# Grouped-query attention on one core: a quarter of the exponentials moves from VectorE to ScalarE, with a check of the row sums and a branch at the end

## The chip, the cores and the metric

The kernel runs on one core of a Trainium2 chip. The metric is device time in microseconds (us); a kernel is run several times and the median counts. The profile is one execution recorded by the hardware profiler: its span runs from the first to the last instruction. The engines are TensorE (PE; its weight loads are listed as PEld), VectorE (DVE), ScalarE (ACT), GpSimd (POOL) and SyncE (SP).

## The reference

Q is 8 x 512 x 32 x 64 (batch, sequence, heads, dimension), K and V have 8 heads of the same length and dimension; all are float32 draws from a unit normal. Four query heads share one key and value head.

```
scores  = einsum('bhqd,bhkd->bhqk', Q, K_expanded) / sqrt(64)
weights = exp(scores - max(scores))
weights = weights / (sum(weights) + 1e-10)
output  = einsum('bhqk,bhkd->bhqd', weights, V_expanded)
```

## The kernel before, in words

There are 32 units: a unit is one batch entry and two key/value heads. GpSimd loads its K, Q and V three units ahead (`emit_load_k` L89, `emit_load_q` L75, `emit_load_v` L101, with a column of ones behind V, L99), converting to bf16. TensorE transposes K and Q of the next unit (L118, L130) into a PSUM buffer, and VectorE copies them out (L120, L134), in three of the four slots of a unit.

A unit has four slots, so there are 128; a slot `p` is one pair of query heads. For each of four chunks `kc` of 128 keys, `emit_scores_chunk` takes a PSUM buffer `s_unit` (128 x 1024 float32, a ring of three, which the transposes share) and makes two matmuls into it (L169), one for each head; the two use different halves of the rows of the array. Then the exponential of the 1024 columns is written as bf16 to the tile `pt`. No row maximum is subtracted. Three of the four chunks go to ScalarE's Exp (L186). The chunk `kc == 1` goes to VectorE (L177): one multiply and add whose result, rounded to a 16-bit integer, is read as the bits of a bf16 number, which approximates the exponential.

`emit_pv_chunk` multiplies the weights of slot `p - 1` with V and accumulates in the single PSUM buffer `pv` (L206, 32 matmuls of 65 columns in a slot); column 65 is the row sum, from the column of ones. `emit_norm` takes reciprocals of the row sums (L223, tile `inv`) and writes the scaled output to `o_sb` (L224). A unit's output is stored by GpSimd during the next unit (L149), the last one at the end.

The loop writes, for each slot: scores 0 and 1, values 0 and 1 of the slot before, scores 2 and 3, values 2 and 3, normalization, transposes. A scheduler orders the instructions of each engine by its own estimate; engines meet through semaphores, and a tile can be written again only when its last reader is done.

Of the kernel before, what the change touches and what calls it, by code (L numbers as in the profile page):

```python
# [10 lines left out]

FP32 = mybir.dt.float32
BF16 = mybir.dt.bfloat16
U16 = mybir.dt.uint16


@with_exitstack
def kernel(
# [7 lines left out]
    nc = tc.nc  # L26

    B, S, H, D = Q.shape
    KV = K.shape[2]
    HPG = H // KV  # L30
    SC = S // 128
# [3 lines left out]
    NSLOT = NU * 2 * NPAIR  # L35

    scale = 1.0 / math.sqrt(D)

    DVE_KC = 1

    SCHRAUD_C = 5.0
    LOAD_PREFETCH = 2
    STORE_DELAY = 2

    A_schr = (2.0 ** 7) / math.log(2.0) * scale
    B_schr = 127.0 * (2.0 ** 7) - SCHRAUD_C

    const_pool = ctx.enter_context(tc.tile_pool(name="const", bufs=1))
    qnat_pool = ctx.enter_context(tc.tile_pool(name="qnat", bufs=LOAD_PREFETCH + 2))
    knat_pool = ctx.enter_context(tc.tile_pool(name="knat", bufs=LOAD_PREFETCH + 2))  # L50
    v_pool = ctx.enter_context(tc.tile_pool(name="v", bufs=LOAD_PREFETCH + 2))
    qt_pool = ctx.enter_context(tc.tile_pool(name="qt", bufs=6))
    kt_pool = ctx.enter_context(tc.tile_pool(name="kt", bufs=3))
    pt_pool = ctx.enter_context(tc.tile_pool(name="pt", bufs=3))
    osb_pool = ctx.enter_context(tc.tile_pool(name="osb", bufs=STORE_DELAY + 2))
    misc_pool = ctx.enter_context(tc.tile_pool(name="misc", bufs=8))

    spsum_pool = ctx.enter_context(tc.tile_pool(name="spsum", bufs=3, space=bass.MemoryType.PSUM))
    pv_pool = ctx.enter_context(tc.tile_pool(name="pv", bufs=1, space=bass.MemoryType.PSUM))

    ident = const_pool.tile([128, 128], BF16)
    make_identity(nc, ident)

    def unit_bgp(u):
        return u // GP, u % GP
# [79 lines left out]
    def emit_store(u, split=False):  # L145
        b, gp = unit_bgp(u)
        h_base = 2 * gp * HPG
        o_sb = pending_stores.pop(u)
        nc.gpsimd.dma_start(  # L149
            out=out[b, :, h_base:h_base + 2 * HPG, :].rearrange(  # L150
                "(sc p) h d -> p sc h d", p=128
            ),
            in_=o_sb,
        )

    jobs = {}
    osb = {}

    def emit_scores_chunk(p, kc):
        st = jobs[p]  # L160
        u, g, i = st["u"], st["g"], st["i"]
        kt_all = trans[u]["kt"]
        qt_tile = trans[u]["qt"][g]
        pt_tile = st["pt"]
        pair_idx = st["pidx"]

        s_unit = spsum_pool.tile([128, 2, S], FP32, name="s_unit")
        for m in range(2):
            nc.tensor.matmul(  # L169
                s_unit[:, m, :],  # L170
                kt_all[64 * m:64 * m + 64, g, kc * 128:(kc + 1) * 128],
                qt_tile[64 * m:64 * m + 64, i, :],
                start=True,
                stop=True,
            )
        if kc == DVE_KC:
            nc.vector.tensor_scalar(  # L177
                out=pt_tile[:, kc, :, :].bitcast(U16),
                in0=s_unit[:, :, :],
                scalar1=float(A_schr),  # L180
                scalar2=float(B_schr),
                op0=mybir.AluOpType.mult,
                op1=mybir.AluOpType.add,
            )
        else:
            nc.scalar.activation(  # L186
                out=pt_tile[:, kc, :, :],
                in_=s_unit[:, :, :],
                func=mybir.ActivationFunctionType.Exp,
                scale=float(scale),  # L190
            )

    def emit_pv_chunk(p, kc):
        st = jobs[p]
# [19 lines left out]
    def emit_norm(p):  # L214
        st = jobs.pop(p)
        u, g, i = st["u"], st["g"], st["i"]
        if u not in osb:
            osb[u] = osb_pool.tile([128, SC, 2, NPAIR, 2, D], FP32, name="o_sb")
            pending_stores[u] = osb[u]
        o_sb = osb[u]  # L220
        o_psums = st["opsums"]
        inv = misc_pool.tile([128, 2, SC], FP32, name="inv")
        nc.vector.reciprocal(out=inv, in_=o_psums[:, :, :, D:D + 1])  # L223
        nc.vector.tensor_tensor(  # L224
            out=o_sb[:, :, g, i, :, :].rearrange("p qc m d -> p m qc d"),
            in0=o_psums[:, :, :, 0:D],
            in1=inv[:, :, :, None].to_broadcast((128, 2, SC, D)),
            op=mybir.AluOpType.mult,
        )
        if st["pidx"] == 2 * NPAIR - 1:  # L230
            osb.pop(u)
# [8 lines left out]
    for p in range(NSLOT + 1):  # L240
        real = p < NSLOT
        if real:
            u, pidx = divmod(p, 2 * NPAIR)
            g, i = divmod(pidx, NPAIR)
# [16 lines left out]
        if real:  # L261
            emit_scores_chunk(p, 0)
            emit_scores_chunk(p, 1)
# [3 lines left out]
        if real:  # L267
            emit_scores_chunk(p, 2)
            emit_scores_chunk(p, 3)
        if have_pv:  # L270
            emit_pv_chunk(p - 1, 2)
            emit_pv_chunk(p - 1, 3)
            emit_norm(p - 1)
# [3 lines left out]
    for w in sorted(pending_stores):  # L277
        emit_store(w, split=True)


# [1 line left out]
_INS = ['Q', 'K', 'V']  # L282
# [26 lines left out]
```

## Time and profile before

| what | value |
|---|---|
| median of 3 runs | 452.14 us (452.01 to 453.33) |
| span of the profiled execution | 449.0 us |
| between the span and the median of the runs | 3.1 us |
| TensorE, VectorE, ScalarE busy | 371.9, 326.0, 367.0 us |
| exponentials on ScalarE | 384, mean 1024 ns each |
| approximations on VectorE | 128, mean 1221 ns each |
| mean granted TensorE clock | 0.995 |

The profile states no other time of the profiled execution than its span; the 3.1 us are the difference of two columns of the table. In a group line the numbers are: busy time and mean duration of one, then the idle time of the engine before such instructions and what ended it. A wait line has the total, the number of waits and the longest. Timeline lines begin with start and length of a run of equal instructions.

### The profile page before, as it was taken

To read this page: it belongs to the slowest core of one execution; us is meant where nothing else is said; L and a number is where in the kernel's file an instruction comes from. 1 tells how busy PE (TensorE), PEld (TensorE's weight loads), DVE (VectorE), ACT (ScalarE), POOL (GpSimd) and SP (SyncE) were. 2 spreads that over 40 slices of the span, in tenths; PEclk is the share of its full clock that TensorE was granted. 3 is DMA by queue.
4 is the path that set the end of the run, shared out by engine and by line. 5 is a ranking of instruction groups with operands and counts; after the bars stand their busy time and mean duration, and the time that the engine had idled before them with its cause. 6 is when DMAs were issued, how large, how long until landed. Compare 5 with 4: busy or idle time off the path is not lost.

```text
span 449.0 us, 13535 instructions
## 1 busy us (share of the span) xinstructions
PE 371.9 (83%) x5888; PEld 219.5 (49%) x5888; DVE 326.0 (73%) x480; ACT 367.0 (82%) x385; POOL 219.0 (49%) x326
## 2 busy tenths in 40 slices
PE   2888888888888888888888888888888888888882
PEld 1445545555455455455554554554545545545541
DVE  1577787777787777778777778777778777777761
ACT  1688888888888888888888888888888888888881
POOL 9988556454456554446645445645445652200000
PEclk9999999999999999999999999999999999999998
DMA  9999999999999999999999999999999999212222
GB/s 90 151 160 213 206 173 148 159 126 121 168 173 147 156 140 113 160 176 149 158 154 110 145 172 165 148 156 128 122 169 172 147 155 157 36 80 96 95 95 93
DMA packets 143930, 63.78 MB, mean 142 GB/s; under 512 B 102912, under 2 KB 135680, under 8 KB 143872
## 3 DMA queue, kind: packets, MB, share of 16 engines
q0 software_dynamic: 143872, 62.93, 95.7%
q8 instruction: 46, 0.75, 0.7%
q14 instruction: 12, 0.10, 0.1%
HBM read 58.72 MB, written 33.55 MB: 206 GB/s over the span
## 4 chain that ended last, share of the span: by engine, by line
PE 65%; issue 13%; ACT 11%; POOL 7%; DMA 1%; ACTq 1%; DVE 0%; POOLq 0%
PE s_unit L169 30%; PE pv L206 28%; ACT pt L186 11%; PE s_unit L130 5%; POOL k_nat L89 3%; PE s_unit L118 3%; POOL q_nat L75 2%; POOL v L101 1%; DMA q_nat<-in_Q_dram 1%; POOL out_dram L149 1%; ACTq L186 1%; DVE pt L177 0%; POOLq L304 0%; POOL v L99 0%; POOL ident masks.py:199 0%
## 5 line engine op out<-in xcount | busy, mean ns | idle before, releaser
L186 ACT ACTIVATE pt<-s_unit 128x1024 bf16<-128x1024 f32 x384 | 365.7, 1024 | 72.5 <-PE s_unit L169 72.5
L169 PE MATMUL s_unit<-qt,kt 64*128 64x512 bf16 x1024 | 191.0, 385 | 60.0 <-ACT pt L186 58.2
L206 PEld LDWEIGHTS <-pt 128*128 128x128 bf16 x4096 | 139.2, 98 | 114.9 <-issue 75.8
L206 PE MATMUL pv<-v,pt 128*128 128x65 bf16 x4096 | 170.3, 195 | 1.0 <-DVE o_sb L224 1.0
L177 DVE TENSOR_SCALAR pt<-s_unit 128x1024 uint16<-128x1024 f32 x128 | 156.3, 1221 | 16.1 <-PE s_unit L169 11.3
L89 POOL DMA_DIRECT2D k_nat<-in_K_dram x128 | 96.7, 783 | 1.2 <-issue 1.1
L224 DVE TENSOR_TENSOR o_sb<-pv,inv 128x512 f32<-128x512 f32 x128 | 88.5, 691 | 4.5
L169 PEld LDWEIGHTS <-kt 64*128 64x128 bf16 x1024 | 40.9, 94 | 97.1 <-issue 78.7
L223 DVE RECIPROCAL inv<-pv 128x8 f32<-128x8 f32 x128 | 26.6, 208 | 83.8 <-PE pv L206 83.8
L75 POOL DMA_DIRECT2D q_nat<-in_Q_dram x64 | 48.2, 766 | 47.1 <-PE s_unit L130 44.9
L99 POOL MEMSET v<- 128x8 bf16 x32 | 4.9, 152 | 122.6 <-PE pv L206 122.6
L101 POOL DMA_DIRECT2D v<-in_V_dram x64 | 47.9, 759 | 4.0 <-DMA q_nat<-in_Q_dram 0.7
L149 POOL DMA_DIRECT2D out_dram<-o_sb x32 | 24.9, 779 | 48.6 <-DVE o_sb L224 48.6
L134 DVE COPY qt<-s_unit 128x1024 bf16<-128x1024 bf16 x64 | 43.5, 679 | 2.4 <-PE s_unit L130 2.4
L130 PE MATMUL s_unit<-ident,q_nat 128*128 128x128 bf16 x512 | 39.9, 222 | 1.8 <-DMA q_nat<-in_Q_dram 1.7
L130 PEld LDWEIGHTS <-q_nat 128*128 128x128 bf16 x512 | 30.3, 99 | 2.4 <-DMA q_nat<-in_Q_dram 2.2
L120 DVE COPY kt<-s_unit 128x1024 bf16<-128x1024 bf16 x32 | 21.8, 680 | 9.5 <-PE s_unit L118 9.5
L118 PE MATMUL s_unit<-ident,k_nat 128*128 128x128 bf16 x256 | 20.5, 225 | 6.6 <-DMA k_nat<-in_K_dram 6.6
L118 PEld LDWEIGHTS <-k_nat 128*128 128x128 bf16 x256 | 15.4, 100 | 7.2 <-issue 5.7
L186 ACT ACT_TABLE_LOAD x1 | 1.3, 1283 | 0.7 <-PEq L293 0.7
masks.py:199 POOL TENSOR_SCALAR_AFFINE_SELECT ident<-ident 128x128 bf16<-128x128 bf16 x1 | 0.3, 305 | 0.1
masks.py:197 POOL MEMSET ident<- 128x128 bf16 x1 | 0.2, 205 | 0.3 <-POOLq L293 0.3
(4 smaller groups left out, 0.4 us busy)
## 6 DMA issues: line engine op xcount, KB each, us to landing
out_dram<-o_sb POOLq DMA_DIRECT2D x32, 1024.0 KB, 5.3
q_nat<-in_Q_dram POOLq DMA_DIRECT2D x64, 256.0 KB, 5.2
k_nat<-in_K_dram POOLq DMA_DIRECT2D x128, 64.0 KB, 4.9
v<-in_V_dram POOLq DMA_DIRECT2D x64, 64.0 KB, 3.1
```

Source lines behind the costliest of these rows:

```text
L75: nc.gpsimd.dma_start(out=q_nat[:, :, g, :, :], in_=Q[b, :, h_base + g * HPG:h_base + (g + 1) * HPG, :].rearrange("(sc p) h d -> p sc h d" ...
L89: nc.gpsimd.dma_start(out=k_nat[:, :, g, c, :], in_=K[b, :, g0 + g, :].rearrange("(sc p) d -> p sc d", p=128),)
L101: nc.gpsimd.dma_start(out=v_tile[:, :, g, 0:D], in_=V[b, :, g0 + g, :].rearrange("(sc p) d -> p sc d", p=128),)
L118: nc.tensor.transpose(kt_ps[:, g, sc, :], k_nat[:, sc, g, :, :], ident)
L130: nc.tensor.transpose(qt_ps[:, i, sc, :], q_nat[:, sc, g, 2 * i:2 * i + 2, :], ident)
L134: nc.vector.tensor_copy(out=qt_tile, in_=qt_ps)
L149: nc.gpsimd.dma_start(out=out[b, :, h_base:h_base + 2 * HPG, :].rearrange("(sc p) h d -> p sc h d", p=128), in_=o_sb,)
L169: nc.tensor.matmul(s_unit[:, m, :], kt_all[64 * m:64 * m + 64, g, kc * 128:(kc + 1) * 128], qt_tile[64 * m:64 * m + 64, i, :], start=True, ...
L177: nc.vector.tensor_scalar(out=pt_tile[:, kc, :, :].bitcast(U16), in0=s_unit[:, :, :], scalar1=float(A_schr), scalar2=float(B_schr), op0=my ...
L186: nc.scalar.activation(out=pt_tile[:, kc, :, :], in_=s_unit[:, :, :], func=mybir.ActivationFunctionType.Exp, scale=float(scale),)
L206: nc.tensor.matmul(o_psums[:, m, qc, :], pt_tile[:, kc, m, qc * 128:(qc + 1) * 128], v_tile[:, kc, g, :], start=(kc == 0 and qc == 0), sto ...
L224: nc.vector.tensor_tensor(out=o_sb[:, :, g, i, :, :].rearrange("p qc m d -> p m qc d"), in0=o_psums[:, :, :, 0:D], in1=inv[:, :, :, None]. ...
```

## The change

All four chunks of a slot go to ScalarE's Exp. The reciprocals of all slots are written to one tile, `inv_all` (128 x 1024). At the end VectorE checks that every reciprocal lies between 2^-60 and 1: in two parts, the columns of all but the last four slots and those of the last four. A one-column matmul counts the partitions that pass, the count is read into a register by every engine, and if it is under 128 a second, general attention with row maxima (`general_path`, a loop over batch entries and heads) computes the whole output anew. With the count at 128 the engines jump over it.

```diff
-        if kc == DVE_KC:
-            nc.vector.tensor_scalar(
-                out=pt_tile[:, kc, :, :].bitcast(U16),
-                in0=s_unit[:, :, :],
-                scalar1=float(A_schr),
-                scalar2=float(B_schr),
-                op0=mybir.AluOpType.mult,
-                op1=mybir.AluOpType.add,
-            )
-        else:
-            nc.scalar.activation(
-                out=pt_tile[:, kc, :, :],
-                in_=s_unit[:, :, :],
-                func=mybir.ActivationFunctionType.Exp,
-                scale=float(scale),
-            )
+        nc.scalar.activation(
+            out=pt_tile[:, kc, :, :],
+            in_=s_unit[:, :, :],
+            func=mybir.ActivationFunctionType.Exp,
+            scale=float(scale),
+        )
...
-        inv = misc_pool.tile([128, 2, SC], FP32, name="inv")
+        inv = inv_all[:, p * 2 * SC:(p + 1) * 2 * SC].rearrange("p (m qc) -> p m qc", m=2)
...
+def check_rows(nc, pool, inv, ok_out):
+    n = inv.shape[1]
+    clamped = pool.tile([128, n], FP32, name="ck_clamp")
+    nc.vector.tensor_scalar(
+        out=clamped, in0=inv, scalar1=float(2.0 ** -60), scalar2=1.0,
+        op0=mybir.AluOpType.max, op1=mybir.AluOpType.min,
+    )
+    same = pool.tile([128, n], FP32, name="ck_same")
+    nc.vector.tensor_tensor(out=same, in0=clamped, in1=inv, op=mybir.AluOpType.is_equal)
+    nc.vector.tensor_reduce(
+        out=ok_out, in_=same, op=mybir.AluOpType.min, axis=mybir.AxisListType.X
+    )
...
+    ones = const_pool.tile([128, 1], FP32)
+    nc.vector.memset(ones, 1.0)
+    inv_all = const_pool.tile([128, NSLOT * 2 * SC], FP32)
...
+    n_all = NSLOT * 2 * SC
+    n_first = n_all - 4 * 2 * SC
+    check_rows(nc, misc_pool, inv_all[:, 0:n_first], ok2[:, 0:1])
+    check_rows(nc, misc_pool, inv_all[:, n_first:n_all], ok2[:, 1:2])
+    nc.vector.tensor_reduce(
+        out=okay, in_=ok2, op=mybir.AluOpType.min, axis=mybir.AxisListType.X
+    )
+    cnt_ps = spsum_pool.tile([128, 2, S], FP32, name="s_unit")[0:1, 0, 0:1]
+    nc.tensor.matmul(cnt_ps, okay, ones, start=True, stop=True)
+    nc.vector.tensor_copy(out=count, in_=cnt_ps)
+    fast.close()
+
+    good = nc.values_load(count[0:1, 0:1], min_val=0, max_val=128)
+    with tc.If(good < 128):
+        general_path(tc, Q, K, V, out, ident)
```

`general_path` works on one key/value head at a time, with 16 tiles of 128 queries each: transposes, one score matmul of 512 columns, a row maximum and a subtraction on VectorE, Exp on ScalarE, a row sum, transposes of the weights, four value matmuls, a scaling.

More of the change, by code (lines that the diff above doesn't have):

```diff
@@ L13 @@
 BF16 = mybir.dt.bfloat16
-U16 = mybir.dt.uint16
+def check_rows(nc, pool, inv, ok_out):
[10 more added lines that the diff above has]
+    )
@@ new lines, in general_path @@
+def general_path(tc, Q, K, V, out, ident):
+    nc = tc.nc
+    B, S, H, D = Q.shape
+    KV = K.shape[2]
+    HPG = H // KV
+    SC = S // 128
+    scale = 1.0 / math.sqrt(D)
+    with ExitStack() as gctx:
+        lp = gctx.enter_context(tc.tile_pool(name="g_load", bufs=2))
+        wp = gctx.enter_context(tc.tile_pool(name="g_work", bufs=2))
+        pp = gctx.enter_context(tc.tile_pool(name="g_psum", bufs=1, space=bass.MemoryType.PSUM))
+        with tc.For_i(0, B, 1) as b, tc.For_i(0, KV, 1) as g:
+            q_nat = lp.tile([128, SC, HPG * D], BF16, name="g_q")
+            k_nat = lp.tile([128, SC, D], BF16, name="g_k")
+            v_nat = lp.tile([128, SC, D], BF16, name="g_v")
+            nc.gpsimd.dma_start(
+                out=q_nat,
+                in_=Q[bass.ds(b, 1), :, bass.ds(g * HPG, HPG), :].rearrange(
+                    "o (sc p) h d -> p (o sc) (h d)", p=128
+                ),
+            )
+            nc.gpsimd.dma_start(
+                out=k_nat,
+                in_=K[bass.ds(b, 1), :, bass.ds(g, 1), :].rearrange(
+                    "o (sc p) h d -> p (o sc) (h d)", p=128
+                ),
+            )
+            nc.gpsimd.dma_start(
+                out=v_nat,
+                in_=V[bass.ds(b, 1), :, bass.ds(g, 1), :].rearrange(
+                    "o (sc p) h d -> p (o sc) (h d)", p=128
+                ),
+            )
+            kt_ps = pp.tile([64, SC, 128], BF16, name="g_ktp")
+            for kc in range(SC):
+                nc.tensor.transpose(kt_ps[:, kc, :], k_nat[:, kc, :], ident)
+            kt = wp.tile([64, S], BF16, name="g_kt")
+            nc.vector.tensor_copy(out=kt, in_=kt_ps.rearrange("p a b -> p (a b)"))
+            o_sb = wp.tile([128, SC, HPG * D], FP32, name="g_o")
+            for h in range(HPG):
+                for qc in range(SC):
+                    qt_ps = pp.tile([64, 128], BF16, name="g_qtp")
+                    nc.tensor.transpose(qt_ps, q_nat[:, qc, h * D:(h + 1) * D], ident)
+                    qt = wp.tile([64, 128], BF16, name="g_qt")
+                    nc.vector.tensor_copy(out=qt, in_=qt_ps)
+                    s_ps = pp.tile([128, S], FP32, name="g_s")
+                    nc.tensor.matmul(s_ps, qt, kt, start=True, stop=True)
+                    mx = wp.tile([128, 1], FP32, name="g_mx")
+                    nc.vector.tensor_reduce(
+                        out=mx, in_=s_ps, op=mybir.AluOpType.max, axis=mybir.AxisListType.X
+                    )
+                    sh = wp.tile([128, S], FP32, name="g_sh")
+                    nc.vector.tensor_scalar(
+                        out=sh, in0=s_ps, scalar1=mx, scalar2=None,
+                        op0=mybir.AluOpType.subtract,
+                    )
+                    p_sb = wp.tile([128, SC, 128], BF16, name="g_p")
+                    nc.scalar.activation(
+                        out=p_sb.rearrange("p a b -> p (a b)"), in_=sh,
+                        func=mybir.ActivationFunctionType.Exp, scale=float(scale),
+                    )
+                    sm = wp.tile([128, 1], FP32, name="g_sm")
+                    nc.vector.tensor_reduce(
+                        out=sm, in_=p_sb.rearrange("p a b -> p (a b)"),
+                        op=mybir.AluOpType.add, axis=mybir.AxisListType.X,
+                    )
+                    nc.vector.tensor_scalar(
+                        out=sm, in0=sm, scalar1=1e-10, scalar2=None, op0=mybir.AluOpType.add
+                    )
+                    iv = wp.tile([128, 1], FP32, name="g_iv")
+                    nc.vector.reciprocal(out=iv, in_=sm)
+                    pt_ps = pp.tile([128, SC, 128], BF16, name="g_ptp")
+                    for kc in range(SC):
+                        nc.tensor.transpose(pt_ps[:, kc, :], p_sb[:, kc, :], ident)
+                    pt = wp.tile([128, SC, 128], BF16, name="g_pt")
+                    nc.vector.tensor_copy(out=pt, in_=pt_ps)
+                    o_ps = pp.tile([128, D], FP32, name="g_ops")
+                    for kc in range(SC):
+                        nc.tensor.matmul(
+                            o_ps, pt[:, kc, :], v_nat[:, kc, :],
+                            start=(kc == 0), stop=(kc == SC - 1),
+                        )
+                    nc.vector.tensor_scalar(
+                        out=o_sb[:, qc, h * D:(h + 1) * D], in0=o_ps, scalar1=iv, scalar2=None,
+                        op0=mybir.AluOpType.mult,
+                    )
+            nc.gpsimd.dma_start(
+                out=out[bass.ds(b, 1), :, bass.ds(g * HPG, HPG), :].rearrange(
+                    "o (sc p) h d -> p (o sc) (h d)", p=128
+                ),
+                in_=o_sb,
+            )
@@ L37 @@
     scale = 1.0 / math.sqrt(D)
-    DVE_KC = 1
-    SCHRAUD_C = 5.0
     LOAD_PREFETCH = 2
     STORE_DELAY = 2
-    A_schr = (2.0 ** 7) / math.log(2.0) * scale
-    B_schr = 127.0 * (2.0 ** 7) - SCHRAUD_C
     const_pool = ctx.enter_context(tc.tile_pool(name="const", bufs=1))
[L49 to L59, printed above, removed]
+    fast = ExitStack()
+    qnat_pool = fast.enter_context(tc.tile_pool(name="qnat", bufs=LOAD_PREFETCH + 2))
+    knat_pool = fast.enter_context(tc.tile_pool(name="knat", bufs=LOAD_PREFETCH + 2))
+    v_pool = fast.enter_context(tc.tile_pool(name="v", bufs=LOAD_PREFETCH + 2))
+    qt_pool = fast.enter_context(tc.tile_pool(name="qt", bufs=6))
+    kt_pool = fast.enter_context(tc.tile_pool(name="kt", bufs=3))
+    pt_pool = fast.enter_context(tc.tile_pool(name="pt", bufs=3))
+    osb_pool = fast.enter_context(tc.tile_pool(name="osb", bufs=STORE_DELAY + 2))
+    misc_pool = fast.enter_context(tc.tile_pool(name="misc", bufs=2))
+    spsum_pool = fast.enter_context(tc.tile_pool(name="spsum", bufs=3, space=bass.MemoryType.PSUM))
+    pv_pool = fast.enter_context(tc.tile_pool(name="pv", bufs=1, space=bass.MemoryType.PSUM))
     ident = const_pool.tile([128, 128], BF16)
     make_identity(nc, ident)
+    ones = const_pool.tile([128, 1], FP32)
+    nc.vector.memset(ones, 1.0)
+    inv_all = const_pool.tile([128, NSLOT * 2 * SC], FP32)
+    okay = const_pool.tile([128, 1], FP32)
+    count = const_pool.tile([1, 1], mybir.dt.int32)
     def unit_bgp(u):
@@ L175, in emit_scores_chunk @@
             )
-        if kc == DVE_KC:
-            nc.vector.tensor_scalar(
-                out=pt_tile[:, kc, :, :].bitcast(U16),
-                in0=s_unit[:, :, :],
-                scalar1=float(A_schr),
-                scalar2=float(B_schr),
-                op0=mybir.AluOpType.mult,
-                op1=mybir.AluOpType.add,
-            )
-        else:
-            nc.scalar.activation(
-                out=pt_tile[:, kc, :, :],
-                in_=s_unit[:, :, :],
-                func=mybir.ActivationFunctionType.Exp,
-                scale=float(scale),
-            )
+        nc.scalar.activation(
+            out=pt_tile[:, kc, :, :],
+            in_=s_unit[:, :, :],
+            func=mybir.ActivationFunctionType.Exp,
+            scale=float(scale),
+        )
     def emit_pv_chunk(p, kc):
@@ L278 @@
         emit_store(w, split=True)
+    ok2 = misc_pool.tile([128, 2], FP32, name="ok2")
+    n_all = NSLOT * 2 * SC
+    n_first = n_all - 4 * 2 * SC
+    check_rows(nc, misc_pool, inv_all[:, 0:n_first], ok2[:, 0:1])
+    check_rows(nc, misc_pool, inv_all[:, n_first:n_all], ok2[:, 1:2])
+    nc.vector.tensor_reduce(
+        out=okay, in_=ok2, op=mybir.AluOpType.min, axis=mybir.AxisListType.X
+    )
+    cnt_ps = spsum_pool.tile([128, 2, S], FP32, name="s_unit")[0:1, 0, 0:1]
[5 more added lines that the diff above has]
+        general_path(tc, Q, K, V, out, ident)
 _INS = ['Q', 'K', 'V']
```

## The prediction

> **What bounds the kernel now.** I read the busy line and the chain on the page, then the groups, then the list of waits, and last the timeline of one slot and of the end.
>
> ```profile
> PE 371.9 (83%) x5888; PEld 219.5 (49%) x5888; DVE 326.0 (73%) x480; ACT 367.0 (82%) x385; POOL 219.0 (49%) x326
> PE 65%; issue 13%; ACT 11%; POOL 7%; DMA 1%; ACTq 1%; DVE 0%; POOLq 0%
> L186 ACT ACTIVATE pt<-s_unit 128x1024 bf16<-128x1024 f32 x384 | 365.7, 1024 | 72.5 <-PE s_unit L169 72.5
> L177 DVE TENSOR_SCALAR pt<-s_unit 128x1024 uint16<-128x1024 f32 x128 | 156.3, 1221 | 16.1 <-PE s_unit L169 11.3
> ```
>
> TensorE and ScalarE are equally busy and VectorE is close behind; no engine is full. The chain runs mostly through TensorE, VectorE has 0% of it. So the 128 VectorE approximations (L177), the work that the change takes away, cost VectorE 156.3 us and the path nothing. The waits tell how the two busy engines stop each other:
>
> ```profile
> ACT pt L186 <- PE s_unit L169: 72.5, 130, 10.1
> PE s_unit L169 <- ACT pt L186: 58.2, 124, 0.5
> ```
>
> 10.1 us of ScalarE's 72.5 are the wait for the first scores; the other 62.4 are 129 waits of 0.48 us, one per slot (a slot is one pair of heads; there are 128). TensorE waits once per slot too, 0.47 us. One slot in the timeline:
>
> ```profile
> 204.90 2.85 ACT L186 ACTIVATE pt<-s_unit 128x1024 bf16<-128x1024 f32 x3 [0.48 <-PE s_unit L169]
> ...
> 206.89 0.39 PE L169 MATMUL s_unit<-qt,kt 64*128 64x512 bf16 x2 [0.46 <-ACT pt L186]
> ...
> 207.21 0.66 PE L206 MATMUL pv<-v,pt 128*128 128x65 bf16 x16
> 207.39 1.22 DVE L177 TENSOR_SCALAR pt<-s_unit 128x1024 uint16<-128x1024 f32 x1 [0.16 <-PE s_unit L169]
> ...
> 207.80 0.61 PE L169 MATMUL s_unit<-qt,kt 64*128 64x512 bf16 x4
> 208.23 2.85 ACT L186 ACTIVATE pt<-s_unit 128x1024 bf16<-128x1024 f32 x3 [0.48 <-PE s_unit L169]
> 208.33 0.53 PEld L206 LDWEIGHTS <-pt 128*128 128x128 bf16 x16 [0.42 <-issue]
> 208.80 0.46 PEld L130 LDWEIGHTS <-q_nat 128*128 128x128 bf16 x8
> ```
>
> A slot lasts 208.23 - 204.90 = 3.33 us. In it ScalarE does three exponentials back to back. Three end 2.85 us after the first begins and one alone lasts 1.02, so they start (2.85 - 1.02) / 2 = 0.913 us apart: the next begins before the one before has been written out. 0.913 is the price of one more exponential in an unbroken row, not 1.024. Three plus the tail of the last (0.11) are 2.85, the wait 0.48: 3.33. The wait arises because the matmul pair at 206.89, held until an exponential ends, feeds VectorE; ScalarE's next scores stand behind it and behind 16 value matmuls, from 207.80.
>
> The end, for the last terms of the sum:
>
> ```profile
> 438.26 1.94 ACT L186 ACTIVATE pt<-s_unit 128x1024 bf16<-128x1024 f32 x2 [0.47 <-PE s_unit L169]
> 440.06 1.16 PE L206 MATMUL pv<-v,pt 128*128 128x65 bf16 x32 [1.03 <-DVE o_sb L224]
> 441.26 0.21 DVE L223 RECIPROCAL inv<-pv 128x8 f32<-128x8 f32 x1 [1.26 <-PE pv L206]
> 441.50 0.69 DVE L224 TENSOR_TENSOR o_sb<-pv,inv 128x512 f32<-128x512 f32 x1
> 442.49 0.75 POOL L149 DMA_DIRECT2D out_dram<-o_sb  x1 [11.37 <-DVE o_sb L224]
> ```
>
> The last exponential ends at 440.20, the last normalization at 442.19, the span at 449.0: the store's issue and landing and the closing barrier.
>
> **Part 1: four exponentials on ScalarE instead of three.** A slot needs at least 4 x 0.913 = 3.65 us of ScalarE, more than the whole slot now (3.33). So ScalarE becomes the bound if TensorE can feed it, and both 0.47 us waits of a slot go only as far as the longer row fills them. Per slot +0.32 us; that, not the 1.22 us that VectorE saves, is the main term. 512 exponentials: 512 x 0.913 = 467.5 us. Bounds: the three-row (0.913) and the two-row of the timeline (1.94 - 1.02 = 0.92): 467 to 471. I take 0.913, the longer row.
>
> [...]
>
> **Can TensorE feed it?** Starts in the timeline: 16 value matmuls take 0.47 us until the next work begins (208.33 to 208.80), a slot has two such groups (0.94); eight transposes 0.57 (208.80 to 209.37, in 96 of 128 slots, so 0.43 on average); a score pair 0.23, four of them 0.9; a change from other matmuls to scores about 0.1 (16 value matmuls take 0.59 before scores, 207.21 to 207.80, against 0.47), up to eight times. Sum 2.3 to 3.1 of 3.65. Longest stretch in the new order before ScalarE gets new scores: 16 value matmuls, eight transposes, one pair: 0.47 + 0.57 + 0.23, and about 0.43 from a pair's start to ScalarE (207.80 to 208.23): 1.7 us. The three s_unit buffers hold one set in work and up to two waiting, 2 x 0.913 = 1.83. It fits, narrowly, and it holds only while transposes do not sit in one of the buffers too long: their copies (0.68 us) now find VectorE free of L177. So I put the steady wait at 0; each 0.1 us per slot would cost 12.8.
>
> **Part 2: the start.** The first exponential begins at 12.11 us, behind loads and transposes that stay; the added memset of ones is on idle VectorE. Between 12.11 and 18.15 ScalarE idles 0.41 + 1.04 + 0.61 = 2.06 us now. One exponential of 0.91 more per slot fills some of it: 1.0, bounds 0 to 2.1.
>
> **Part 3: the end until the store.** In the order of the changed kernel the last slot's value matmuls need not wait as a block of 32; only the last eight (0.24) stand behind the last exponential. From its end to the reciprocal: 0.05 + 0.24 + 0.2 = 0.5 instead of 441.26 - 440.20 = 1.06. So 449.0 - 440.2 - 0.6 = 8.2 us from the last exponential to the end.
>
> **Part 4: the certificate.** Reciprocals write into one tile: same work. The first check (three VectorE operations over 992 columns; near rows 0.68 for a 1024 copy and 1.22 for L177: 2.0 to 3.7 us) stands in VectorE's queue ahead of the fourth normalization from the end, which has to free the only pv buffer. VectorE has 0.9 us of normalization in those slots of 3.65, so 0 to 1 us comes through; I take 0. The second check starts when the last normalization is done: four small VectorE operations (0.1 to 0.21, the reciprocal's row), a one-column matmul, a copy, hand-overs of 0.05: 0.9 to 1.8 us. Meanwhile the last store lands 4 to 5 us after its issue, so this is covered. Then all five engines load the count, compare and jump, twice. The trace has no such load or jump. Lowest: sequencer work of 0.1, all under the store: 0. Highest: a load as dear as a DMA's issue to landing (5.3, page part 6) and two jumps each fetching 16 KB of instructions (packets of queue 8 took 0.9 to 1.6): 1.8 + 5.3 + 3.2 = 10.3 after the normalization, against 5.7 (447.9) at which GpSimd's closing drain ends now: +4.6; if that drain starts over behind it, some 5 more. The queued work behind the load is only that drain and the barrier, for which all engines wait. I take +2, between, nearer to the packets.
>
> [...]
>
> **Sum.** 12.1 + 467.5 + 0.1 (tail of the last) + 1.0 + 8.2 + 2.0 = 490.9 us of span against 449.0. Around the span lie 452.14 - 449.0 = 3.1 (median of the runs shown; the profiled span is the only time of that execution). Predicted 494.0 us, 9% slower.
>
> **Rivals.**
> *ScalarE starves at the ring.* Place: L186 behind the pair that follows transposes. For it: the wait exists now, once per slot, and my margin is 0.1 us. Against: it hangs today on the pair for VectorE, which is gone. Price: 0.48 us in each of 96 slots, 46 us: 540; in one slot of four 15 us: 509. Chance 0.10.
> *The branch is dear.* Both jumps, the load and a repeated drain exposed: 4.6 to 10 instead of 2: 497 to 502. Chance 0.12. Small in effect, it is part of the range.
> *Exponentials get faster once VectorE stops reading PSUM beside them* (the side of faster). Place: L186. If ScalarE runs at half rate beside the 1.22 us of L177, three exponentials lose 0.6 us, one 0.2: 0.71 x 512 = 364, total 390. It decides from (452.1 - 26.5) / 512 = 0.831 us apart. Against: all 384 exponentials lie between 1017 and 1032 ns, beside L177 or not. Chance 0.03.
> *The general path runs.* A row sum outside 1 to 2^60 would be needed; 512 exponentials of scores with unit spread sum to hundreds. 1024 tiles at some us each, milliseconds. Chance 0.01.
>
> **Numbers.** The forecast has 0.74. Its own range, from spacing (467 to 471), start (-1 to +1), end (-2 to +3): 490 to 500. The dear branch ends at 502, the mild starving at 509; I cut at 506. The low end 488 allows a spacing 1% under the row's. A run of this kernel can tell 0.3% (1.4 us) from no change; only the third rival gets there: 0.02 beyond the strip and 0.01 within it. Faster 0.02, same 0.01, slower 0.97.
>
> **What would show it.** Right: L186 x512, near 470 us busy, its idle after the first exponential a few us; starts 3.65 us apart per slot; VectorE near 175 us busy; TensorE's wait for ScalarE grown well over 58.2. Wrong: idle on L186 <- PE s_unit of tens of us (ring), spacing other than 0.91 (first term), or a gap of over 5 us between the last store's landing and the end (branch).

## The result and the profile after

The changed kernel takes 493.98 us (median of 4 runs, 493.68 to 494.17) against 452.74 us (452.01 to 453.39, 4 runs) of the kernel before: ratio 1.092, 95% interval 1.090 to 1.094, so 41 us slower. The forecast was 494.0 us, with a range of 488 to 506. The profiled execution took 493.68 us with a span of 492.0.

First the busy line, the chain and the groups of the page of the changed kernel (Exp is now L291, the score matmuls L284).

```profile
span 492.0 us, 13447 instructions
PE 396.0 (80%) x5890; PEld 253.9 (52%) x5890; DVE 176.6 (36%) x361; ACT 470.7 (96%) x513; POOL 219.1 (45%) x326
ACT 90%; PE 3%; issue 2%; DMA 1%; POOL 1%; DVE 1%; POOLq 0%
L291 ACT ACTIVATE pt<-s_unit 128x1024 bf16<-128x1024 f32 x512 | 469.4, 1302 | 10.4 <-PE s_unit L284 10.4
```

ScalarE went from 82% to 96% of a longer span and from 11% to 90% of the chain; VectorE fell from 326 to 176.6 us, and that bought nothing. The 10.4 us of idle are the wait for the first scores, and the list of waits shows the whole exchange:

```profile
PE s_unit L284 <- ACT pt L291: 72.1, 217, 0.5
ACT pt L291 <- PE s_unit L284: 10.4, 1, 10.4
```

ScalarE waits once in 492 us. The 129 waits of 0.48 us are gone, and TensorE waits for ScalarE oftener (217 times, before 124). Two stretches of ScalarE's timeline show the price of one exponential:

```profile
12.71 12.02 ACT L291 ACTIVATE pt<-s_unit 128x1024 bf16<-128x1024 f32 x13 [10.44 <-PE s_unit L284]
...
479.73 2.43 ACT L291 ACTIVATE pt<-s_unit 128x1024 bf16<-128x1024 f32 x2
```

The first 13 take 12.02 us: (12.02 - 1.02) / 12 = 0.917 us each. The last ends at 479.73 + 2.43 = 482.16, so the row lasts 482.16 - 12.71 = 469.45 us, 0.917 for each of 512: without one gap, from start to end. A slot is 3.67 us, before 3.33 to 3.34.

### The profile page after: what moved, and what is told of

It is laid out like the page before. It is cut to its first block, busy times and chain, and to the rows that moved or that the text cites. A ratio compares the mean times of both kernels' runs of the same rounds, so it can differ in the third digit from the quotient of the medians.

```text
span 492.0 us, 13447 instructions
## 1 busy us (share of the span) xinstructions
PE 396.0 (80%) x5890; PEld 253.9 (52%) x5890; DVE 176.6 (36%) x361; ACT 470.7 (96%) x513; POOL 219.1 (45%) x326
## 4 chain that ended last, share of the span: by engine, by line
ACT 90%; PE 3%; issue 2%; DMA 1%; POOL 1%; DVE 1%; POOLq 0%
ACT pt L291 90%; PE s_unit L284 3%; DMA q_nat<-in_Q_dram 1%; POOL k_nat L204 1%; PE pv L311 0%; DVE o_sb L329 0%; PE s_unit L245 0%; POOL q_nat L190 0%; DVE inv_all L328 0%; POOL ident masks.py:199 0%; PE s_unit L394 0%; POOL ident masks.py:197 0%; DVE ck_same L30 0%; DVE ok L31 0%; DVE okay L390 0%
## 5 line engine op out<-in xcount | busy, mean ns | idle before, releaser
L291 ACT ACTIVATE pt<-s_unit 128x1024 bf16<-128x1024 f32 x512 | 469.4, 1302 | 10.4 <-PE s_unit L284 10.4
L284 PE MATMUL s_unit<-qt,kt 64*128 64x512 bf16 x1024 | 191.4, 383 | 75.3 <-ACT pt L291 72.1
L311 PEld LDWEIGHTS <-pt 128*128 128x128 bf16 x4096 | 144.3, 98 | 107.3 <-issue 61.4
L311 PE MATMUL pv<-v,pt 128*128 128x65 bf16 x4096 | 186.4, 195 | 2.1 <-DVE o_sb L329 1.2
L328 DVE RECIPROCAL inv_all<-pv 128x8 f32<-128x8 f32 x128 | 26.6, 208 | 290.1 <-PE pv L311 290.1
L284 PEld LDWEIGHTS <-kt 64*128 64x128 bf16 x1024 | 65.8, 93 | 109.3 <-issue 81.0
L329 DVE TENSOR_TENSOR o_sb<-pv,inv_all 128x512 f32<-128x512 f32 x128 | 88.5, 692 | 4.4
L190 POOL DMA_DIRECT2D q_nat<-in_Q_dram x64 | 48.1, 761 | 63.6 <-PE s_unit L245 62.4
L264 POOL DMA_DIRECT2D out_dram<-o_sb x32 | 25.0, 781 | 53.4 <-DVE o_sb L329 41.2
L245 PEld LDWEIGHTS <-q_nat 128*128 128x128 bf16 x512 | 34.3, 98 | 4.1 <-DMA q_nat<-in_Q_dram 2.3
L30 DVE TENSOR_TENSOR ck_same<-ck_clamp,inv_all 128x992 f32<-128x992 f32 (+1 forms) x2 | 1.4, 692 | 0.1
L31 DVE TENSOR_REDUCE ok<-ck_same 128x1 f32<-128x992 f32 (+1 forms) x2 | 1.4, 686 | 0.1
```

Source lines behind the costliest of these rows:

```text
L190: nc.gpsimd.dma_start(out=q_nat[:, :, g, :, :], in_=Q[b, :, h_base + g * HPG:h_base + (g + 1) * HPG, :].rearrange("(sc p) h d -> p sc h d" ...
L245: nc.tensor.transpose(qt_ps[:, i, sc, :], q_nat[:, sc, g, 2 * i:2 * i + 2, :], ident)
L264: nc.gpsimd.dma_start(out=out[b, :, h_base:h_base + 2 * HPG, :].rearrange("(sc p) h d -> p sc h d", p=128), in_=o_sb,)
L284: nc.tensor.matmul(s_unit[:, m, :], kt_all[64 * m:64 * m + 64, g, kc * 128:(kc + 1) * 128], qt_tile[64 * m:64 * m + 64, i, :], start=True, ...
L291: nc.scalar.activation(out=pt_tile[:, kc, :, :], in_=s_unit[:, :, :], func=mybir.ActivationFunctionType.Exp, scale=float(scale),)
L311: nc.tensor.matmul(o_psums[:, m, qc, :], pt_tile[:, kc, m, qc * 128:(qc + 1) * 128], v_tile[:, kc, g, :], start=(kc == 0 and qc == 0), sto ...
```

## The experiments

The theory to be tested was: ScalarE's row is the new bound, 0.917 us an exponential; what lies at the end costs some 1.5 us; everything else is covered. The rivals: the certificate costs more than the end shows; TensorE is at its limit too.

**The certificate alone.** Chunk 1 goes back to VectorE in the changed kernel.

```diff
-        nc.scalar.activation(
+        if kc == 1:
+            nc.vector.tensor_scalar(
...
+        else:
+            nc.scalar.activation(
```

> The certificate, the load of the count and the branch of the changed kernel, with the exponentials as before (chunk 1 on VectorE). Theory (the exponentials on ScalarE are the whole cost but for some 1.5 us at the end): 454.3 us, between 453.5 and 455.5, that is before + 0.8 to + 2.8; 384 exponentials, one wait of 0.48 us in each slot as before. Rival (the shared tile of reciprocals, the checks on VectorE or the jump cost more than the end shows): 457 us or over.

Measured: 455.4 us (453.57 to 457.27), ratio 1.009 to the kernel before (1.006 to 1.013). As a time this lies in the theory's range, but the kernel before took 451.48 us in the same rounds, so the certificate adds 3.9 us: more than the theory's 0.8 to 2.8, and a little less than the rival's 4.3 and over. The branch costs what it costs in the changed kernel: from the last normalization to the end of the span lie 8.4 us in both (454.0 - 445.56 here), 6.8 before. The rest comes with the first check, in VectorE's timeline of this kernel:

```profile
432.50 0.67 DVE L26 TENSOR_SCALAR ck_clamp<-inv_all 128x992 f32<-128x992 f32 x1
433.20 1.19 DVE L31 TENSOR_TENSOR ck_same<-ck_clamp,inv_all 128x992 f32<-128x992 f32 x1
434.31 0.20 DVE L339 RECIPROCAL inv_all<-pv 128x8 f32<-128x8 f32 x1
434.59 1.23 DVE L293 TENSOR_SCALAR pt<-s_unit 128x1024 uint16<-128x1024 f32 x1
435.73 0.68 DVE L340 TENSOR_TENSOR o_sb<-pv,inv_all 128x512 f32<-128x512 f32 x1
436.32 1.17 DVE L32 TENSOR_REDUCE ok<-ck_same 128x1 f32<-128x992 f32 x1
```

The check's 3.03 us stand between approximations that a slot needs, with no idle time left in the brackets. The last normalization ends 4.8 us after the last exponential here (445.56 against 440.79), 2.0 before. Not all of these 2.8 us are the check. ScalarE waits less in this run (61.7 us after its first wait, before 62.4), and its exponentials take 427.3 us from first to last instead of 428.1. And the last block of value matmuls ran at a lower clock than the same block of the slot before:

```profile
440.58 1.17 PE L322 MATMUL pv<-v,pt 128*128 128x65 bf16 x32 [1.52 <-DVE o_sb L340]
442.77 1.81 PE L322 MATMUL pv<-v,pt 128*128 128x65 bf16 x32 [1.03 <-DVE o_sb L340]
```

The granted clock was 1.00 until 442 us and 0.50 from 443.5 to 446; that is 0.6 us. From the first exponential to the last normalization this kernel takes 2.0 us more than the one before (432.1 against 430.1), so some 1.4 us are left for the check itself, by this one execution. In the changed kernel the same three operations stand in a VectorE that is 36% busy, and ScalarE's row has no gap there. So the check is hidden by the time that the moved work has left free on VectorE, and by that estimate it costs some 1.4 us where VectorE still does its share. That reading comes from the traces; no run moved the check.

**The exponentials alone.** The kernel before with every chunk on ScalarE; no certificate, no branch.

```diff
-        if kc == DVE_KC:
+        if False:
```

> All exponentials on ScalarE, nothing of the certificate and no branch. Theory: 492.4 us (491.5 to 493.2): the changed kernel less the 1.6 us between its and the old end. Rival (certificate dear): 489 or less.

Measured: 492.47 us (492.13 to 493.15), ratio 1.091 (1.089 to 1.094). The theory holds. The exponentials alone add 41.0 us to the kernel before of the same rounds (451.48), and the changed kernel added 41.2 in its own; by the times of the two changed kernels, which come from different rounds, they differ by 1.5. So 40 to 41 of the 41 us are the exponentials.

**The branch, without what it jumps over, and taken out.** In the first kernel the loops of the general path run once; in the second the loads of the count, the branch and the path are gone and the checks stay.

```diff
-            for h in range(HPG):
-                for qc in range(SC):
+            for h in range(1):
+                for qc in range(1):
```

> The changed kernel with the general path cut to one query tile of one head, so that fewer TensorE and VectorE instructions are jumped over (that path is not entered with these inputs). Theory (the 5.5 us that TensorE spends in its branch are the fetch of instructions that lie beyond what it holds): TensorE's branch under 1 us, VectorE's too, the end then set by GpSimd's drain behind the last store, 492.9 us (1.1 less than the changed kernel). Rival (a jump costs this whatever lies between): branch still 5 us, 494.0 us.

```diff
-    good = nc.values_load(count[0:1, 0:1], min_val=0, max_val=128)
-    with tc.If(good < 128):
-        general_path(tc, Q, K, V, out, ident)
```

> The changed kernel with its certificate computed but without the loads of the count, the branch and the general path. Theory (the 1.5 us between the changed kernel and the one without a certificate are the branch: 0.8 us more until GpSimd's drain is over and 1.0 until TensorE has fetched; the checks are hidden): 492.4 us (491.8 to 493.0). Rival (the checks themselves hold up the end): 493.5 us or more.

Measured: 493.44 us (493.11 to 493.78) and 492.54 us (492.53 to 493.03). The first time lies halfway between theory and rival and decides nothing; the second is the theory's. The branch's own line in the changed kernel, then in the one with the short path (min, median and longest duration in ns, start):

```profile
L399 PEldq COMPARE_BRANCH  x1: 5493/5493/5493, 485.5 to 485.5; - x1
```

```profile
L399 PEldq COMPARE_BRANCH  x1: 358/358/358, 486.4 to 486.4; - x1
```

The jump costs TensorE 5.49 us over the general path, whose loop body has 164 matmuls and transposes, and 0.36 over the short one with 14, so the cost goes with the length of the code that is skipped, and the rival falls. From the last exponential to the end of the span: 492.02 - 482.16 = 9.86 us in the changed kernel, 8.63 with the short path, 8.44 without a branch, 8.23 without a certificate. The long jump is worth 1.2 us of span, the rest of branch and checks 0.4. The times of whole runs show the order of the first three, but their steps (0.5 and 0.9 us) are blurred by the first exponential, which began between 12.7 and 13.2 us in these four profiles.

**Half an exponential less in each slot.** Chunk 1's exponential covers half its columns.

```diff
+        cols = S // 2 if kc == 1 else S
         nc.scalar.activation(
-            out=pt_tile[:, kc, :, :],
-            in_=s_unit[:, :, :],
+            out=pt_tile[:, kc, :, 0:cols],
+            in_=s_unit[:, :, 0:cols],
...
-                    pt_tile[:, kc, m, qc * 128:(qc + 1) * 128],
+                    pt_tile[:, 0 if kc == 1 and qc >= SC // 2 else kc, m, qc * 128:(qc + 1) * 128],
```

> The changed kernel in which the exponential of chunk 1 covers only half of its columns; the value matmuls of the other half read chunk 0's weights, so TensorE's work is unchanged. Theory (ScalarE's row is the only bound, TensorE feeds it with room to spare): an exponential of 512 columns ends 0.49 us after the one before, a slot takes 3 x 0.917 + 0.49 = 3.24 us, the time falls by 128 x 0.427 = 55 us to 439. Rival (the three buffers are at their limit, TensorE's order takes over as soon as the row shortens): slots of 3.33 us or more, 451 us or over.

Measured: 451.76 us (451.02 to 452.27), ratio to the kernel before 1.001 (0.999 to 1.002). My theory lost here and the rival was right: the gain stops at the old slot time. TensorE's timeline in this kernel:

```profile
203.61 0.39 PE L284 MATMUL s_unit<-qt,kt 64*128 64x512 bf16 x2 [0.44 <-ACT pt L292]
203.93 0.66 PE L312 MATMUL pv<-v,pt 128*128 128x65 bf16 x16
204.52 0.60 PE L284 MATMUL s_unit<-qt,kt 64*128 64x512 bf16 x4
...
206.94 0.39 PE L284 MATMUL s_unit<-qt,kt 64*128 64x512 bf16 x2 [0.46 <-ACT pt L292]
```

206.94 - 203.61 = 3.33 us, the slot of the kernel before, with the same stations: the end of chunk 3's exponential frees a score buffer; the held pair for chunk 1 (203.61); 16 value matmuls; at 204.52 the pair for chunk 2, 0.91 later; 0.44 of hand-over; the exponentials of chunks 2 and 3, 1.94 by the timeline of before; 0.04 until the next held pair. Together 3.33. The engine that does chunk 1, VectorE or ScalarE with half the columns, is not in that loop. The busy line and the waits do not tell this. ScalarE is 95% busy, and hardly a wait is recorded:

```profile
ACT pt L292 <- PE s_unit L284: 11.3, 2, 11.0
```

The lost time hides in the overlap of the row. The exponential of chunk 2 starts at 204.96, 0.44 us after its pair and just as the short one ends (204.96), so it ends 1.01 us after its predecessor instead of 0.92. This 0.1 us per slot is all that parts theory (3.24) and rival (3.33). ScalarE alone could also lose it behind a short exponential, and this run does not exclude that outright. For the pair speaks that in 122 of the 127 slots with a next one the exponential of chunk 2 starts 0.41 to 0.43 us after the last score matmul before it, as in the kernel before (0.43), and that the slot is the old one to 0.01 us. The four exponentials of the changed kernel (3.67) outlast the loop by 0.33 us per slot: that is the reserve by which TensorE feeds ScalarE. The short exponential itself behaved as expected: by the recorded ends, it ended 0.490 us after its predecessor, against 0.917 for a whole one, 0.83 ns per column.

**Two score buffers.** The changed kernel with the ring of three cut to two.

```diff
-    spsum_pool = fast.enter_context(tc.tile_pool(name="spsum", bufs=3, space=bass.MemoryType.PSUM))
+    spsum_pool = fast.enter_context(tc.tile_pool(name="spsum", bufs=2, space=bass.MemoryType.PSUM))
```

> The changed kernel with two score buffers instead of three. This makes the case of the rival in which ScalarE starves: a pair can be made only while one exponential runs. Theory (three buffers leave a reserve of 3.67 - 3.33 us per slot, two leave none): idle of ScalarE before L291 over 50 us, 540 to 590 us. If two buffers were enough, 494 us.

Measured: 555.7 us (two runs). The group of the exponentials:

```profile
L291 ACT ACTIVATE pt<-s_unit 128x1024 bf16<-128x1024 f32 x512 | 479.3, 1042 | 62.7 <-PE s_unit L284 62.7
```

The theory holds, and this is the starving that the rival described: 62.7 us of idle against 10.4, each with the wait for the first scores, and a mean duration back at 1.04 us, since each wait breaks the row.

**A loop that is cut.** If the old slot is that loop, it can be shortened without moving any exponential to another engine. Two kernels, each one edit to the kernel before: another chunk on VectorE, or another place for the value matmuls.

```diff
-    DVE_KC = 1
+    DVE_KC = 2
```

> The kernel before with chunk 2 instead of chunk 1 on VectorE. Theory (the old slot of 3.33 us is a loop: chunk 3's exponential ends, TensorE's held pair for chunk 1, 16 value matmuls, the pair for chunk 2, its hand-over, the exponentials of chunks 2 and 3; with chunk 2 on VectorE one exponential leaves that loop): slots under 3.28 us, 441 us (435 to 446), ScalarE's idle below 50 us. Rival (the slot is the sum of work that TensorE and ScalarE do in turn, whichever chunk VectorE takes): 451 us.

```diff
         if real:
             emit_scores_chunk(p, 0)
+        if have_pv:
+            emit_pv_chunk(p - 1, 0)
+        if have_pv:
+            emit_pv_chunk(p - 1, 1)
+        if real:
             emit_scores_chunk(p, 1)
-        if have_pv:
-            emit_pv_chunk(p - 1, 0)
-            emit_pv_chunk(p - 1, 1)
         if real:
             emit_scores_chunk(p, 2)
+        if have_pv:
+            emit_pv_chunk(p - 1, 2)
+        if have_pv:
+            emit_pv_chunk(p - 1, 3)
+        if real:
             emit_scores_chunk(p, 3)
         if have_pv:
-            emit_pv_chunk(p - 1, 2)
-            emit_pv_chunk(p - 1, 3)
             emit_norm(p - 1)
```

> The kernel before (chunk 1 on VectorE) with the loop written as scores 0, values 0 and 1, scores 1 and 2, values 2 and 3, scores 3. Theory of the loop (the 16 value matmuls no longer stand between the pairs of chunks 1 and 2): 439 us (433 to 446). Rival (sum of work): 451 us.

Measured: 419.28 us (418.8 to 419.56), ratio 0.928 (0.926 to 0.931), and 421.10 us (420.67 to 421.93), ratio 0.932 (0.930 to 0.935). Both beat the kernel before and the changed one, and by more than I expected: both times lie below the ranges that the theory of the loop gave (435 to 446 and 433 to 446), by 14 us and more. From the page of the first:

```profile
PE 365.0 (87%) x5888; PEld 236.4 (57%) x5888; DVE 318.9 (76%) x480; ACT 365.0 (87%) x385; POOL 218.8 (52%) x326
PE 40%; DVE 39%; issue 16%; POOL 2%; DMA 1%; DVEq 0%; POOLq 0%
L186 ACT ACTIVATE pt<-s_unit 128x1024 bf16<-128x1024 f32 x384 | 363.7, 1029 | 42.6 <-PE s_unit L169 25.1
```

The engines do nearly the same work (365 us of ScalarE, 319 of VectorE; before 367 and 326), but ScalarE idles 42.6 us instead of 72.5, and a slot takes 3.09 us ((408.34 - 12.66) / 128, first start to last end of the exponentials). The chain now alternates between TensorE and VectorE. Why 3.09 and not 3.25 I did not work out. Both kernels rule out that the old slot was a sum of work: with the same work it depends on the order. They fit the loop, whose stations I read from the timelines, but not the price that I put on its parts.

## Why the prediction was right

Term by term, against the profiled execution of 493.68 us:

| term | predicted | measured |
|---|---|---|
| first exponential begins | 12.1 | 12.7 |
| row of 512, its tail and start gaps | 468.6 | 469.4 |
| from the last exponential to the end | 8.2 + 2.0 | 8.2 + 1.6 |
| around the span | 3.1 | 1.7 |
| sum | 494.0 | 493.7 |

The mechanism is shown: the exponentials alone carry 40 to 41 of the 41 us, and the trace has one row without a gap. The closeness of the sum is partly luck, since the terms missed by up to 1.9 us and cancelled.

The row: 0.913 was read from rounded rows of three and is 0.917, 1.9 us more over 512. The division as I wrote it, (2.85 - 1.02) / 2, gives 0.915 and not 0.913, and so does the mean over the rows of three in the trace of before; with it the row would have missed by 0.9 us. The start gaps that I put at 1.0 did not occur, since the first 13 exponentials run without one; that took back about half of the 1.9.

The end: without a certificate it is 8.23 us, as predicted, though the path differed. The last 32 value matmuls still stand as one block, but they begin while the last exponential runs, and the reciprocal comes 0.51 us after it (482.67 against 482.16). The count's load, for which I had allowed up to 5.3 us, took 0.46 to 0.76 us; the second check was covered; and each engine jumps once, not twice. The part that showed is the jump: 5.49 us on TensorE, more than my bound of 1.6 per jump from the instruction packets. That TensorE fetches instructions in this time was my supposition, in that bound and in the theories of the two kernels on the branch; the runs show that the time goes with the length of the path (5.49 and 0.36 us), but not that a fetch is the reason: in the 5.49 us the trace has one 16 KB packet of instructions (0.98 us) and three of 8 KB (under 0.5 us each), the first from 488.2 on, and the short path has one of each too, after its jump was done. The jump cost just 1.2 us of span because GpSimd's drain behind the last store was running until 490.06 anyway, 0.8 us later after its store than before (6.16 against 5.40). Without the branch it ends 5.60 us after its store, so most of the delay comes with the count's load (0.55 us on GpSimd) and the branch.

Around the span: 3.1 was the median of runs less the span of one execution. In the profiles that have both numbers the difference is 1.6 to 1.9 (493.68 - 492.02 here). So the term was too large by 1.4 us: by this difference the profiled execution of before took some 450.7 us, less than any of the runs that I took the median of. That error offset those of the start and the row.

Weakest step: the question whether TensorE can feed. I added up its work and a longest stretch, and found a margin of 0.1 us in a buffer's time. The conclusion held, but what decides is the loop through the held pair, whose 3.33 us were in the timeline that I quoted, and the reserve is 0.33 us per slot. Seeing that would have given the reserve and the result of the halved exponential, and would have pointed to the faster kernels, though not to how fast they are. The rival of starving did not occur; two buffers show it is real. The third rival fell too: without VectorE beside it, an exponential costs 0.917, in the rows of three before 0.915. The general path did not run.

## What to carry to other kernels

When work moves to an engine whose waits come from a loop and not from lack of work, price it by the unbroken row on that engine (start of the first to end of the last, over the count), and compare it with the loop: here the larger one set the slot, and the waits did not add. Before giving an engine's work away because the path does not show it, walk one period of the timeline from wait to wait and write down which instruction holds which; here the better change was to take one station out of that loop. Count a branch over much code at the end of a kernel as a term of its own: here it took 5.49 us on TensorE, which has the longest code in the part that is skipped, and 1.2 us of that showed in the span, since GpSimd's drain behind the last store ran beside it.

## What the runs showed of the hardware

In the changed kernel the recorded durations of exponentials grew along the unbroken row, from 1.02 to 1.53 us; in the short rows of the kernel before they lay between 1.017 and 1.032. The tile's view of the changed kernel (shortest, median and longest duration in ns):

```profile
L291 ACT ACTIVATE pt<-s_unit x512: 1018/1303/1526, 12.7 to 480.6; 128x1024 bf16<-128x1024 f32 x171
```

By the trace's records, they mostly start 0.904 us apart and end 0.917 apart, so each is recorded about 0.013 us longer than the one before, up to 1.53 us; a start that comes later takes some of that back. A mean of 1302 ns against 1024 is therefore no slower exponential; the ends tell the rate. The jump over the general path took TensorE 5.49 us, while ScalarE, GpSimd and SyncE, with at most 16 operations each in that path, took 0.05 us. VectorE, with 129, has its branch recorded with 0.07 us, but its next instruction comes 4.6 us later (490.3 against 485.6); with the short path it comes 0.5 us later (487.1 against 486.6).
